# A dense mixture of experts on TensorE: 112 gathered tokens instead of 96, and the gathered sums on GpSimd

## The chip, the cores and the metric

The kernel runs on one core of one Trainium2 chip. The time is device microseconds (us) from the start to the end of one execution. The engines are PE (TensorE: matrix products), DVE (VectorE), ACT (ScalarE), POOL (GpSimd) and SP (SyncE, which here only issues DMAs). Each engine runs its own list of instructions in order; they wait for each other through semaphores.

## What is computed

The reference is two transformer-like blocks on 512 tokens of width 1024. The change sits almost wholly in the first block's expert layer. There are 16384 experts of one neuron each; every token picks 128 of them (8 heads, 16 each), and sums their outputs by a gate:

```python
    def block_fn(args):
        hb, ib, gb = args
        u = expert_down[ib]
        act = jax.nn.gelu(jnp.einsum("td,thkd->thk", hb, u), approximate=False)
        v = expert_up[ib]
        return jnp.einsum("thk,thkd->td", gb * act, v)
```

`hb` are the tokens, `ib` their expert numbers, `gb` the gates. The second block has, among other things, a linear attention, a state-space layer (S5) and a feed-forward layer.

## The kernel before

**Two ways to do the experts.** For most tokens (TD = 416) the kernel does all 16384 experts densely, as 128 blocks j of 128 experts, and multiplies by a gate that is zero for experts not picked. For the first TG = 96 tokens it gathers only the picked experts' rows from memory. `GROUPS` lists the gathered tokens as (first token, number of gathers, picks of a token in one gather): (0, 64, 2) and (64, 32, 4). Each gather fetches 128 rows of 1024 floats, 512 KB.

**Down stage** (loop over j, L815 to L826). `linear` loads the block `ed[j]`, splits it into a high and a low part (`hi` by ACT at L118, `lo` by DVE at L119; each in three buffers), and issues 24 matmuls of 128 x TD (L126, L127, L128). ACT applies the GELU and every second block goes to memory as `act_d`. After each block `run_fill` takes pieces of other work from a list: `select` (the top-k, on DVE), `scatter` (the dense gates of 8 tokens: three one-hot operations on DVE at L734, L737, L740, 16 matmuls at L745, ACT copies, and for every TC = 32 tokens a POOL DMA into `g_d`), `dot` (POOL gathers a `row` at L756, three buffers; DVE multiplies it with the tokens and sums, L764), `weigh` (GELU of the dots times gate) and the first NOW = 16 `add`s. An `add` gathers a row of `expert_up` on POOL (L756, the same three buffers) and DVE does `tsum += row * gate` in one instruction (L779).

**Up stage** (loop over j, L1050 to L1097). Per block ACT loads `aj` (two blocks of `act_d`) and for every eight blocks `gt` (their gates from `g_d`); `load_w` brings `eu[j]`; DVE forms `wg = aj * gt` (L1077), ACT and DVE split it into `wh` and `wl` (L131, L132), and 24 matmuls of 128 x 416 add into eight PSUM banks. The other 80 `add`s and the preparation of the second block (`s5_prepare`, `ada`) are in this stage's list. The last two blocks are held back, and after them small matmuls (L1097) add `tsum`.

**What sets the order.** A scheduler places the instructions of each engine; `soon()` gives the weight path priority, `issue_after` holds an instruction until a named one is issued, and `fill`'s costs and budgets say how much goes beside each block. What stands in the list of an engine is then run strictly in that order.

**Second block.** At L1397 SP loads the S5 inputs `u4` (8 DMAs for each of 8 parts) in the same queue as the weights; `tables` (L1403) and `carry` (L1435) are called in turn in the loop at L1493 to L1520.

## Time and profile before

| what | us |
|---|---|
| median of three runs (lowest, highest) | 2742.34 (2730.85, 2746.29) |
| the profiled execution | 2736.44 |
| its span in the trace | 2734.7 |
| PE busy | 2630.8 (96%) |
| DVE busy | 1874.4 (69%) |
| ACT busy | 1070.8 (39%) |
| POOL busy | 491.1 (18%) |
| down stage, 423 to 1102 us | 679 |
| up stage, 1107 to 1720 us | 613 |

The profiled execution's mean granted PE clock was 0.983 of full speed. Busy time of PE counts pipelined matmuls, so the distance between the starts of two matmuls, not the duration of one, is what a matmul costs. POOL's DMA issues count as busy where they are indirect (gathers). The rows are in a section of their own below.

### The profile page before, as it was taken

Reading aid. Unit: us, or ns where it says so; the run is one execution under the profiler, and the core shown is the slowest. Engines: PE = TensorE matmul, PEld = TensorE weight load, DVE = VectorE, ACT = ScalarE, POOL = GpSimd, SP = SyncE. Lnnn points to the kernel's source line nnn. Section 1 sums busy time; section 2 is a strip of 40 time slices with the busy share of each in tenths; the row PEclk is TensorE's granted clock in tenths of the full one; section 3 lists DMA queues with packets and bytes.
Section 4 is the critical chain, followed back from the end, with each engine's and each line's share of the span. In section 5 each row is a group of like instructions: output and inputs, shape, how many; then the busy total and the mean of one; then the engine's idle time right before and its main releaser. Section 6 shows DMA issues by size and latency. Waiting matters only on the chain.

```text
span 2734.7 us, 36390 instructions
## 1 busy us (share of the span) xinstructions
PE 2630.8 (96%) x13784; PEld 2349.5 (86%) x13784; DVE 1874.4 (69%) x3430; ACT 1070.8 (39%) x1510; POOL 491.1 (18%) x431
## 2 busy tenths in 40 slices
PE   6999999999999999999999899999999989999997
PEld 5777789999999999999899899877788878688886
DVE  5777699998998874788688576744456654562543
ACT  4564333434445444334433233544323243432221
POOL 0001000343343021224423120100002320010100
PEclk9999999999999999999999999999999999999999
DMA  6324424889888577979887887222265654233321
GB/s 255 101 87 139 144 93 133 282 286 327 301 307 323 188 263 259 313 273 339 297 319 265 281 302 258 82 63 70 70 193 177 191 159 132 72 98 96 97 96 66
DMA packets 182304, 532.95 MB, mean 195 GB/s; under 512 B 20592, under 2 KB 59472, under 8 KB 180208
## 3 DMA queue, kind: packets, MB, share of 16 engines
q1 hardware_dynamic: 89872, 282.57, 31.2%
q0 software_dynamic: 39952, 157.64, 16.5%
q10 hardware_dynamic: 52304, 90.41, 9.7%
q8 instruction: 108, 1.77, 0.3%
q14 instruction: 68, 0.56, 0.1%
HBM read 448.98 MB, written 80.41 MB: 194 GB/s over the span
## 4 chain that ended last, share of the span: by engine, by line
PE 84%; DMA 6%; DVE 5%; issue 2%; ACT 2%; POOL 1%; ACTq 0%; SPq 0%; DVEq 0%; POOLq 0%
PE ps L127 24%; PE ps L126 24%; PE ps L128 24%; PE ps L745 4%; DMA gt<-g_d 3%; DMA row<-in_eu_dram,gid 1%; DVE lo L119 1%; PE ps L1307 1%; PE ps L1310 1%; DVE wg L1077 1%; PE ps L615 1%; PE ps L148 0%; PE ps L1421 0%; ACT hi L118 0%; PE ps L487 0%
## 5 line engine op out<-in xcount | busy, mean ns | idle before, releaser
L118 ACT ACTIVATE hi<-raw 128x1024 fp32r<-128x1024 f32 (+2 forms) x459 | 481.3, 1051 | 1068.0 <-PE ps L127 796.9
L119 DVE TENSOR_TENSOR lo<-raw,hi 128x1024 fp32r<-128x1024 f32 (+2 forms) x459 | 579.4, 1264 | 347.6 <-ACT hi L118 319.1
L126 PE MATMUL ps<-h2h,hi 128*128 128x416 f32 (+1 forms) x1152 | 413.1, 360 | 3.9 <-ACT h2h L569 3.0
L127 PE MATMUL ps<-h2l,hi 128*128 128x416 f32 (+1 forms) x1152 | 413.1, 359 | 2.9 <-DVE h2l L570 2.9
L128 PE MATMUL ps<-h2h,lo 128*128 128x416 f32 (+1 forms) x1152 | 411.2, 358 | 0.0
L127 PE MATMUL ps<-wl,hi 128*128 128x416 f32 x1024 | 363.8, 355 | 11.4 <-DVE wl L132 11.4
L128 PE MATMUL ps<-wh,lo 128*128 128x416 f32 x1024 | 358.4, 357 | 10.9 <-DVE lo L119 10.9
L126 PE MATMUL ps<-wh,hi 128*128 128x416 f32 x1024 | 351.2, 355 | 6.6 <-ACT wh L131 4.5
L126 PE MATMUL ps<-Ah,hi 128*128 128x512 f32 (+2 forms) x944 | 337.7, 363 | 18.0 <-ACT Ah L131 7.0
L127 PE MATMUL ps<-Al,hi 128*128 128x512 f32 (+2 forms) x944 | 340.6, 361 | 2.7 <-DVE Al L1123 2.7
L128 PE MATMUL ps<-Ah,lo 128*128 128x512 f32 (+2 forms) x944 | 338.1, 359 | 0.5 <-DVE lo L119 0.5
L756 POOL DMA_INDIRECT row<-in_eu_dram,gid x96 | 181.9, 1895 | 398.5 <-DVE tsum L779 329.6
L126 PEld LDWEIGHTS ps<-h2h,hi 128*128 128x128 f32 x1152 | 218.0, 189 | 11.5 <-ACT h2h L569 3.8
L127 PEld LDWEIGHTS ps<-h2l,hi 128*128 128x128 f32 x1152 | 217.8, 189 | 9.9 <-DVE h2l L570 3.6
L128 PEld LDWEIGHTS ps<-h2h,lo 128*128 128x128 f32 x1152 | 217.8, 189 | 6.4
L126 PEld LDWEIGHTS ps<-Ah,hi 128*128 128x128 f32 x944 | 179.0, 191 | 50.0 <-ACT Ah L131 7.9
L127 PEld LDWEIGHTS ps<-wl,hi 128*128 128x128 f32 x1024 | 194.4, 190 | 16.6 <-DVE wl L132 13.0
L127 PEld LDWEIGHTS ps<-Al,hi 128*128 128x128 f32 x944 | 180.2, 191 | 32.6 <-issue 5.0
L128 PEld LDWEIGHTS ps<-wh,lo 128*128 128x128 f32 x1024 | 195.5, 191 | 13.1 <-DVE lo L119 11.9
L128 PEld LDWEIGHTS ps<-Ah,lo 128*128 128x128 f32 x944 | 179.6, 190 | 30.7 <-issue 6.0
L126 PEld LDWEIGHTS ps<-wh,hi 128*128 128x128 f32 x1024 | 196.0, 192 | 10.2 <-ACT wh L131 5.2
L756 POOL DMA_INDIRECT row<-in_ed_r_dram,gid x96 | 144.6, 1506 | 218.9 <-DVE dots L764 194.1
(602 smaller groups left out, 4199.5 us busy)
## 6 DMA issues: line engine op xcount, KB each, us to landing
raw<-in_ed_dram SPq DMA_DIRECT2D x128, 512.0 KB, 5.1
raw<-in_eu_dram SPq DMA_DIRECT2D x128, 512.0 KB, 5.5
raw<-in_win_dram SPq DMA_DIRECT2D x67, 512.0 KB, 3.6
raw<-in_wff_dram SPq DMA_DIRECT2D x64, 512.0 KB, 3.8
g_d<-gst POOLq DMA_DIRECT2D x13, 2048.0 KB, 9.7
aj<-act_d ACTq DMA_DIRECT2D x64, 416.0 KB, 4.5
wa<-in_wada_dram SPq DMA_DIRECT2D x46, 512.0 KB, 4.5
gt<-g_d ACTq DMA_DIRECT2D x45, 512.0 KB, 9.8
```

The lines of the kernel that those rows point to most:

```text
L118: top[0] = nc.scalar.activation(hi[:, :n], raw[:, :n], AF.Copy)
L119: low[0] = nc.vector.tensor_sub(lo[:, :n], raw[:, :n], hi[:, :n].bitcast(F32))
L126: nc.tensor.matmul(ps, wh, x[0], start=first, stop=False)
L127: nc.tensor.matmul(ps, wh, x[1], start=False, stop=False)
L128: nc.tensor.matmul(ps, wl, x[0], start=False, stop=last)
L615: nc.tensor.matmul(ps[:, t * P : t * P + P], q[:, t * P : t * P + P], skt[:, m], start=True, stop=True)
L745: nc.tensor.matmul(ps[:, i * P : i * P + P], o1[:, c, :, i], o2[a][:, c, :, i], start=a == 0, stop=a == 1)
L756: nc.gpsimd.indirect_dma_start(out=raw, out_offset=None, in_=src.rearrange("a b d -> (a b) d"), in_offset=bass.IndirectOffsetOnAxis(ap=gid ...
L1077: nc.vector.tensor_tensor(wg.rearrange("p (c t) -> p c t", t=TC), aj[:, j % 2].rearrange("p (c t) -> p c t", t=TC), gt[:, :, j % 8], ALU.mult)
L1307: nc.tensor.matmul(po[hs], qx[:, c * 64 : c * 64 + 64], st, start=False, stop=True)
L1310: nc.tensor.matmul(ps, kt[hs, j], vt[hs, j], start=True, stop=True)
```

## The change

**Groups and widths.** A third group (96, 16, 8) is gathered, so TG is 112 and TD 400. The gates are kept by TC = 24 tokens: 400 = 16 x 24 + 16, in 16 chunks of `g_d` and one smaller `ge_d`. `wg` becomes two DVE instructions (384 and 16 columns), `gt` gets a fifth, small DMA and is issued after the block j-8 instead of j-6.

**Sums.** An `add` is now a POOL gather, a POOL multiplication in place (`row * gate`) and a POOL addition (`tsum += row`), carried out one or two gathers after its own. No sum is left on DVE. NOW is 48: of these, 32 alternate with the dots of groups 1 and 2, and 16 come after all the dots. 64 stay for the up stage. `weigh(1)` and `weigh(2)` come after all the dots.

**The rest.** The first `aj` goes into two buffers of another pool (tag "tl", which the dots' `junk` uses too) through SP; `fill`'s budget goes over P-6 blocks with a cap of 4.8 instead of P-8 and 4.2; in S5 the `u4` loads go from SP's queue to POOL's, and `tables` is called after `carry`.

```diff
-    TC = 32
-    GROUPS = ((0, 64, 2), (64, 32, 4))
+    TC = 24
+    GROUPS = ((0, 64, 2), (64, 32, 4), (96, 16, 8))
...
-    NCH = TD // TC
+    NCH, TE = divmod(TD, TC)
...
+    ge_d = dp.tile([P, P, TE], F32, name="ge_d")
...
-            if i == 0:
-                tsum[g] = gx.tile([P, D], F32, tag=f"tok{g}", name=f"tsum{g}")
-                nc.vector.tensor_scalar(tsum[g], raw, w, None, ALU.mult)
-            else:
-                nc.vector.scalar_tensor_tensor(tsum[g], raw, w, tsum[g], ALU.mult, ALU.add)
...
+        def sums_of(lag):
+
+            while len(pending) > lag:
+                g, i, raw = pending.pop(0)
+                w = ggate[g][:, i : i + 1]
+                if g not in tsum:
+                    tsum[g] = gx.tile([P, D], F32, tag=f"tok{g}", name=f"tsum{g}")
+                    nc.gpsimd.tensor_scalar(tsum[g], raw, w, None, ALU.mult)
+                else:
+                    nc.gpsimd.tensor_scalar(raw, raw, w, None, ALU.mult)
+                    nc.gpsimd.tensor_tensor(tsum[g], tsum[g], raw, ALU.add)
+
+        def add(g, i, lag):
+            pending.append((g, i, fetch(I["eu"], g, i)))
+            sums_of(lag)
...
-        SPILL, NOW = 0, 16
+        NOW, LAST = 48, 16
+        adds = [(1.3, lambda p=p, n=n: add(*p, 1 if n < NOW else 2)) for n, p in enumerate(picks)]
...
+        down = [dot_of(p) for p in picks[:n0]] + [(0.1, lambda: weigh(0))]
+        dots_, adds_ = [dot_of(p) for p in picks[n0:]], adds[: NOW - LAST]
+        while dots_ or adds_:
+            for l in (dots_, adds_):
+                if l:
+                    down.append(l.pop(0))
+        down += [(0.1, lambda g=g: weigh(g)) for g in range(1, len(GROUPS))]
...
-        fill.extend(down)
-
-        per = sum(c for c, _ in fill) / (P - 8)
+        fill.extend(down + adds[NOW - LAST : NOW] + [(0.1, lambda: sums_of(0))])
+
+        per = sum(c for c, _ in fill) / (P - 6)
...
-            run_fill(min((j + 1) * per - done[0], 4.2))
+            run_fill(min((j + 1) * per - done[0], 4.8))
...
+            gathers = adds[NOW:] + [(0.1, lambda: sums_of(0))]
...
-                with tc.issue_after(tops[max(j - 6, 0)].ins) if j else ExitStack():
+                with tc.issue_after(tops[max(j - 8, 0)].ins) if j else ExitStack():
...
+                    nc.scalar.dma_start(ge[:, a:b], ge_d[:, j // 8 * 8 + a : j // 8 * 8 + b])
...
+                if j == 0:
+                    aj = [tp.tile([P, TD], F32, tag="tl", name=nm("aj"), bufs=3) for _ in range(2)]
+                    for i, a in enumerate(aj):
+                        nc.sync.dma_start(a, act_d[0][:, i * TD : i * TD + TD])
...
-                nc.vector.tensor_tensor(
-                    wg.rearrange("p (c t) -> p c t", t=TC), aj[:, j % 2].rearrange("p (c t) -> p c t", t=TC), gt[:, :, j % 8], ALU.mult)
+                v = lambda a: a[:, : NCH * TC].rearrange("p (c t) -> p c t", t=TC)
+                nc.vector.tensor_tensor(v(wg), v(aj[j % 2]), gt[:, :, j % 8], ALU.mult)
+                nc.vector.tensor_tensor(wg[:, NCH * TC :], aj[j % 2][:, NCH * TC :], ge[:, j % 8], ALU.mult)
...
-                        nc.sync.dma_start(u4[r0 : r0 + 16, 4 * m : 4 * m + 4], usrc[g, s])
+                        nc.gpsimd.dma_start(u4[r0 : r0 + 16, 4 * m : 4 * m + 4], usrc[g, s])
...
-            if gi % 2 == 0 and gi + 2 < NGR:
-                nxt = tables(gi // 2 + 1)
             if gi % 2 == 1:
                 sts = nxt
             cur, held = held, carry(gi + 1, sts) if gi + 1 < NGR else None
+            if gi % 2 == 0 and gi + 2 < NGR:
+                nxt = tables(gi // 2 + 1)
```

**DVE, from the down stage to the up stage.** In the kernel before, the list of DVE there reads as follows (`lo_10037` to `lo_10115` belong to the first three blocks of the up stage):

```order
L119 TENSOR_TENSOR lo_10037<-raw_10035,hi_10036 128x1024
L119 TENSOR_TENSOR lo_10073<-raw_10071,hi_10072 128x1024
L1077 TENSOR_TENSOR wg_10041<-aj_10033,gt_10028 128x416
L1077 TENSOR_TENSOR wg_10077<-aj_10033,gt_10028 128x416
L1031 TENSOR_REDUCE fold_10024<-ident 128x64
L1031 TENSOR_REDUCE fold_10026<-ident 128x32
L119 TENSOR_TENSOR lo_10115<-raw_10113,hi_10114 128x1024
L132 TENSOR_TENSOR wl_10043<-wg_10041,wh_10042 128x416
L132 TENSOR_TENSOR wl_10079<-wg_10077,wh_10078 128x416
L1077 TENSOR_TENSOR wg_10119<-aj_10111,gt_10028 128x416
```

The first `wg` stand behind weight splits alone. In the changed kernel (`lo_10166` is the last block of the down stage; `lo_10232`, `lo_10269` and `lo_10313` are the first three of the up stage; L767 is a dot, in two instructions) the list reads:

```order
L119 TENSOR_TENSOR lo_10166<-raw_10164,hi_10165 128x1024
L119 TENSOR_TENSOR lo_10232<-raw_10230,hi_10231 128x1024
L767 ISA junk_8833,dots_2368<-row_8831,htok_2365 128x1024
L767 ISA dots_2368 128x1
L119 TENSOR_TENSOR lo_10269<-raw_10267,hi_10268 128x1024
L1041 TENSOR_REDUCE fold_10214<-ident 128x64
L1041 TENSOR_REDUCE fold_10216<-ident 128x32
L1041 TENSOR_REDUCE fold_10218<-ident 128x16
L119 TENSOR_TENSOR lo_10313<-raw_10311,hi_10312 128x1024
L767 ISA junk_8903,dots_2368<-row_8901,htok_2365 128x1024
L767 ISA dots_2368 128x1
L767 ISA junk_9005,dots_2368<-row_9003,htok_2365 128x1024
```

and, 30 instructions further on, with the last of the third group's dots ahead:

```order
L767 ISA junk_9695,dots_2372<-row_9693,htok_2369 128x1024
L767 ISA dots_2372 128x1
L767 ISA junk_9761,dots_2372<-row_9759,htok_2369 128x1024
L767 ISA dots_2372 128x1
L771 TENSOR_TENSOR ggate_2371<-ggate_2371,dots_2372 128x16
L1091 TENSOR_TENSOR wg_10236<-aj_10226,gt_10220 128x384
L1092 TENSOR_TENSOR wg_10236<-aj_10226,gt_10220 128x16
L132 TENSOR_TENSOR wl_10238<-wg_10236,wh_10237 128x400
```

Between `lo_10313` and the first `wg` there now stand 18 dots (two of group 1, all 16 of group 2) and the instructions of `weigh`.

**POOL, at the same place.** In the changed kernel, the last gathers of the down stage (L759; `in_ed_r` for a dot, `in_eu` for a sum), with the multiplications (L786) and additions (L787) among them:

```order
L759 DMA row_9003<-in_ed_r_dram,gid_2366 128x1024
L759 DMA row_9069<-in_eu_dram,gid_2362 128x1024
L786 TENSOR_SCALAR row_8966<-row_8966,ggate_2363 128x1024
L759 DMA row_9073<-in_ed_r_dram,gid_2370 128x1024
L786 TENSOR_SCALAR row_9069<-row_9069,ggate_2363 128x1024
L787 TENSOR_TENSOR tsum_6630<-tsum_6630,row_8966 128x1024
L759 DMA row_9139<-in_ed_r_dram,gid_2370 128x1024
L759 DMA row_9176<-in_ed_r_dram,gid_2370 128x1024
L787 TENSOR_TENSOR tsum_6630<-tsum_6630,row_9069 128x1024
L759 DMA row_9241<-in_ed_r_dram,gid_2370 128x1024
L759 DMA row_9245<-in_ed_r_dram,gid_2370 128x1024
```

A sum's multiplication of `row_9069` stands behind its own gather and ahead of all but one of the third group's gathers (`gid_2370`).

**POOL, in the up stage.** Before, POOL only gathers there, and issues the DMAs of the S5 preparation (`mats_d`):

```order
L756 DMA row_11428<-in_eu_dram,gid_2361 128x1024
L756 DMA row_11467<-in_eu_dram,gid_2361 128x1024
L985 DMA mats_d<-bd_10195 128x8x128
L985 DMA mats_d<-bd_10196 128x8x128
L756 DMA row_11595<-in_eu_dram,gid_2361 128x1024
L985 DMA mats_d<-bd_10195 128x8x128
L985 DMA mats_d<-bd_10196 128x8x128
L756 DMA row_11598<-in_eu_dram,gid_2361 128x1024
L756 DMA row_11637<-in_eu_dram,gid_2361 128x1024
```

Now, gathers, multiplications and additions follow each other:

```order
L759 DMA row_9939<-in_eu_dram,gid_2362 128x1024
L759 DMA row_9943<-in_eu_dram,gid_2362 128x1024
L786 TENSOR_SCALAR row_9902<-row_9902,ggate_2363 128x1024
L787 TENSOR_TENSOR tsum_6630<-tsum_6630,row_9902 128x1024
L786 TENSOR_SCALAR row_9939<-row_9939,ggate_2363 128x1024
L759 DMA row_9947<-in_eu_dram,gid_2362 128x1024
L786 TENSOR_SCALAR row_9943<-row_9943,ggate_2363 128x1024
L787 TENSOR_TENSOR tsum_6630<-tsum_6630,row_9939 128x1024
L786 TENSOR_SCALAR row_9947<-row_9947,ggate_2363 128x1024
L787 TENSOR_TENSOR tsum_6630<-tsum_6630,row_9943 128x1024
L759 DMA row_9984<-in_eu_dram,gid_2362 128x1024
L787 TENSOR_TENSOR tsum_6630<-tsum_6630,row_9947 128x1024
```

The addition of a row stands up to two rows behind its gather; the multiplication is often right behind one.

## Rows read from the trace of the kernel before

**Rows 1.** Windows: stretch, length, busy us (x instructions) by engine, PE clock, DMA share, GB/s.

```profile
423.00:1102.00 679.00, 678.13 (x3922) 658.43 (x3921) 566.17 (x952) 307.43 (x385) 188.82 (x142) 1.00 0.77 270
1102.00:1107.00 5.00, 0.86 (x5) 0.52 (x3) 1.05 (x3) 1.48 (x2) 0.00 (x0) 0.82 0.84 284
1107.00:1720.00 613.00, 588.19 (x3049) 577.62 (x3050) 468.06 (x776) 212.69 (x292) 174.80 (x97) 0.98 0.85 291
```

**Rows 2.** Chain that ended last: start us, length us, what; four of its pieces.

```profile
956.81 1.91 PE ps L745 x16
...
1102.90 3.03 DMA aj<-act_d
...
1519.59 27.26 DMA row<-in_eu_dram,gid
...
1610.71 17.51 DMA gt<-g_d
```

**Rows 3.** Timeline of PE in the up stage: start us, us, instruction; eight issues apart.

```profile
1129.65 0.35 PE L128 MATMUL ps<-wh,lo 128*128 128x416 f32 x1
...
1131.15 0.35 PE L127 MATMUL ps<-wl,hi 128*128 128x416 f32 x1
```

**Rows 4.** The same view at 512 columns, eight issues apart.

```profile
2299.73 0.39 PE L128 MATMUL ps<-Ah,lo 128*128 128x512 f32 x1
...
2301.54 0.39 PE L127 MATMUL ps<-Al,hi 128*128 128x512 f32 x1
```

**Rows 5.** Groups by line, whole span: count | busy us, mean ns | idle before, releaser.

```profile
L756 POOL DMA_INDIRECT row<-in_eu_dram,gid x96 | 181.9, 1895 | 398.5 <-DVE tsum L779 329.6 <-DMA row<-in_eu_dram,gid 14.2 <-DVE s5e L876 14.0
...
L756 POOL DMA_INDIRECT row<-in_ed_r_dram,gid x96 | 144.6, 1506 | 218.9 <-DVE dots L764 194.1 <-DVE pi L666 8.9 <-issue 4.6
...
L764 DVE CUSTOM_DVE_ANT_0 junk<-row,htok 128x1024 bf16<-128x1024 f32 x96 | 116.0, 1218 | 21.4 <-DMA row<-in_ed_r_dram,gid 21.3
...
L950 POOL MEMSET bd<- 128x1024 f32 x2 | 1.9, 984 | 0.0
```

**Rows 6.** The same grouping for DVE in the up stage alone, 1107 to 1720 us.

```profile
L779 DVE SCALAR_TENSOR_TENSOR tsum<-row,ggate,tsum 128x1024 f32<-128x1024 f32 x79 | 100.9, 1278 | 15.9 <-DMA row<-in_eu_dram,gid 15.9
...
L1077 DVE TENSOR_TENSOR wg<-aj,gt 128x416 f32<-128x416 f32 x127 | 69.7, 584 | 50.3 <-DMA gt<-g_d 36.9 <-issue 9.2 <-DMA aj<-act_d 4.1
...
L219 DVE DVE_READ_ACCUMULATOR2_ANT mod<- 128x1 f32 x8 | 0.7, 82 | 0.0
```

**Rows 7.** Timelines of PE, ACT and DVE where the down stage ends and up begins.

```profile
1102.52 0.34 PE L128 MATMUL ps<-h2h,lo 128*128 128x416 f32 x1
...
1107.18 2.10 PE L126 MATMUL ps<-wh,hi 128*128 128x416 f32 x5 [4.32 <-ACT wh L131]
...
1103.35 1.06 ACT L118 ACTIVATE hi<-raw 128x1024 fp32r<-128x1024 f32 x1 [3.65 <-PE ps L128]
...
1105.95 1.09 DVE L1077 TENSOR_TENSOR wg<-aj,gt 128x416 f32<-128x416 f32 x2 [5.40 <-DMA aj<-act_d]
```

**Rows 8.** Timelines of POOL and DVE in the feed-forward stage: start us, us, instruction.

```profile
2437.77 1.04 POOL L1591 TENSOR_TENSOR f<-f 128x512 f32<-128x512 f32 x1 [4.40 <-ACT hi L118]
...
2437.80 2.09 DVE L119 TENSOR_TENSOR lo<-raw,hi 128x1024 fp32r<-128x1024 f32 x1 [0.18 <-ACT hi L118]
...
2465.18 1.23 DVE L119 TENSOR_TENSOR lo<-raw,hi 128x1024 fp32r<-128x1024 f32 x1 [4.24 <-ACT hi L118]
```

**Rows 9.** DMA issues: queue, count, KB each, median us from issue to landing.

```profile
raw<-in_ed_dram SPq DMA_DIRECT2D x128, 512.0 KB, 5.1
...
gt<-g_d ACTq DMA_DIRECT2D x45, 512.0 KB, 9.8
...
row<-in_ed_r_dram,gid POOLq DMA_INDIRECT x96, 6.9
...
row<-in_eu_dram,gid POOLq DMA_INDIRECT x96, 8.0
```

**Rows 10.** Chain again, at the start of the second block's S5 stage.

```profile
2026.26 1.08 SPq L1397
...
2028.84 3.94 DMA raw<-in_win_dram
```

More of the change, by code (lines that the diff above doesn't have):

```diff
@@ L727, in scatter @@
             if off == 0:
-                gst[ch] = px.tile([P, P, TC], F32, tag="g", name=nm("gst"))
+                gst[ch] = px.tile([P, P * TC], F32, tag="g", name=nm("gst"))
+            tc_ = TC if ch < NCH else TE
+            to = gst[ch][:, : P * tc_].rearrange("p (j t) -> p j t", t=tc_)
             n = SC // 4
@@ L746, in scatter @@
                 nc.scalar.copy(
-                    gst[ch][:, :, off + 4 * c : off + 4 * c + 4].rearrange("p j t -> p t j"), ps.rearrange("p (t j) -> p t j", j=P))
-            if off + SC == TC:
-                nc.gpsimd.dma_start(g_d[ch], gst[ch])
+                    to[:, :, off + 4 * c : off + 4 * c + 4].rearrange("p j t -> p t j"), ps.rearrange("p (t j) -> p t j", j=P))
+            if off + SC == tc_:
+                nc.gpsimd.dma_start(g_d[ch] if ch < NCH else ge_d, to)
         picks = [(g, i) for g, (_, n, _) in enumerate(GROUPS) for i in range(n)]
@@ L770, in tile_blocks @@
         tsum = {}
-        def add(g, i):
-            raw = fetch(I["eu"], g, i)
-            w = ggate[g][:, i : i + 1]
-            if i == 0:
-                tsum[g] = gx.tile([P, D], F32, tag=f"tok{g}", name=f"tsum{g}")
-                nc.vector.tensor_scalar(tsum[g], raw, w, None, ALU.mult)
-            else:
-                nc.vector.scalar_tensor_tensor(tsum[g], raw, w, tsum[g], ALU.mult, ALU.add)
-        def later(fn):
-            with tc.issue_after(low[0].ins):
-                fn()
+        pending = []
+        def sums_of(lag):
[11 more added lines that the diff above has]
+            sums_of(lag)
         dot_of = lambda p: (1.4, lambda p=p: dot(*p))
-        adds = [(1.3, lambda p=p: later(lambda: add(*p))) for p in picks]
-        SPILL, NOW = 0, 16
+        NOW, LAST = 48, 16
+        adds = [(1.3, lambda p=p, n=n: add(*p, 1 if n < NOW else 2)) for n, p in enumerate(picks)]
         select(0)
@@ L797, in tile_blocks @@
         todo, fill[:] = fill[:], []
-        dotted = []
-        for g, (_, n, _) in enumerate(GROUPS):
-            dotted += [dot_of(p) for p in picks if p[0] == g]
-            dotted.append((0.1, lambda g=g: weigh(g)))
-        cut = len(dotted) - SPILL - 1 if SPILL else len(dotted)
-        down, left = dotted[:cut], dotted[cut:]
-        down += adds[:NOW]
+        n0 = GROUPS[0][1]
+        down = [dot_of(p) for p in picks[:n0]] + [(0.1, lambda: weigh(0))]
[5 more added lines that the diff above has]
+        down += [(0.1, lambda g=g: weigh(g)) for g in range(1, len(GROUPS))]
         share = sum(c for c, _ in down) / sum(c for c, _ in todo)
@@ L1040, in beside @@
             fill.clear()
-            of_first = GROUPS[0][1]
-            gathers = []
-            for i, a in enumerate(adds[NOW:of_first]):
-                gathers.append(a)
-                if left and i % 2 == 1:
-                    gathers.append(left.pop(0))
-            gathers += left + adds[max(of_first, NOW) :]
+            gathers = adds[NOW:] + [(0.1, lambda: sums_of(0))]
             share = sum(c for c, _ in gathers) / sum(c for c, _ in rest)
@@ L1067, in tile_blocks @@
                         nc.scalar.dma_start(gt[:, c:c1, a:b], g_d[c:c1, :, j // 8 * 8 + a : j // 8 * 8 + b].rearrange("c p j t -> p c j t"))
+                    nc.scalar.dma_start(ge[:, a:b], ge_d[:, j // 8 * 8 + a : j // 8 * 8 + b])
             if j % 2 == 0:
-                aj = px.tile([P, 2, TD], F32, tag="act", name=nm("aj"))
-                nc.scalar.dma_start(aj.rearrange("p a t -> p (a t)"), act_d[j // 2])
+                if j == 0:
+                    aj = [tp.tile([P, TD], F32, tag="tl", name=nm("aj"), bufs=3) for _ in range(2)]
+                    for i, a in enumerate(aj):
+                        nc.sync.dma_start(a, act_d[0][:, i * TD : i * TD + TD])
+                else:
+                    at_ = px.tile([P, 2, TD], F32, tag="act", name=nm("aj"))
+                    nc.scalar.dma_start(at_.rearrange("p a t -> p (a t)"), act_d[j // 2])
+                    aj = [at_[:, i] for i in range(2)]
             w = load_w(I["eu"][j])
```

4 lines of the change are left out of this document (3 added, 1 removed).

## The prediction

> **What bounds the kernel now.** I read the windows first. In the down stage (423 to 1102 us) PE is busy for 678 of 679 us, DVE for 566 and POOL for 189; in the up stage PE for 588 of 613, DVE for 468 and POOL for 175 [rows 1]. So PE sets both stages, and DVE is the next engine. How much a matmul costs is the distance of two starts: eight take 1131.15 - 1129.65 = 1.50 us at 416 columns, 0.1875 each [rows 3]. A stage has 128 x 24 = 3072 of them, 576 us. In the down stage 832 scatter matmuls at 1.91 / 16 = 0.119 [rows 2] add 99, in all 675 of 679. In the up stage 613 - 576 = 37 us are not matmul pace. The chain shows where most of it goes: gate tiles that landed late (17.5 us for `gt<-g_d` at 1610) and once a gathered row for which DVE waited (27 us at 1519) [rows 2]. Between the stages PE stands still from 1102.52 to 1107.18, 4.67 us, because the first `wg` waits for `aj` [rows 2, 7].
>
> **The narrower dense part (a gain).** At 512 columns eight matmuls take 1.81 us, 0.2263 each [rows 4]. The slope is (0.2263 - 0.1875) / 96 = 0.0004 us a column; 16 columns are 0.0065 us, by plain proportion 0.0072, so 20 to 22 us in each stage: 21. Two scatters fewer are 32 x 0.119 = 4 us, down only. That is -25 in the down stage and -21 in the up stage before anything is late, on PE, which sets both ends.
>
> **The price of a sum on POOL.** DVE did it in 1.28 us [rows 6]. Now POOL does two instructions on 128x1024. An addition of 128x512 took POOL 1.04 us [rows 8], so 2.08 at twice the size. A multiplication by one value a row has no row on POOL: it lies between a fill of the same size, 0.98 [rows 5], and the addition's 2.08. I take 1.1, nearest to the fill, since it has one input where the addition has two. A sum is 3.2 us (3.06 to 4.16).
>
> **POOL holds DVE up.** In the feed-forward stage a weight split on DVE that starts 0.03 us behind a POOL addition takes 2.09 us, and 1.23 where POOL is idle; it ends 1.08 us after the addition's end, as if it had begun only then [rows 8]. Nearly all of DVE's work in both stages (weight splits, dots, `wg`, `wl`) also has two inputs in SBUF. So I count POOL's additions, and its multiplications too, as time taken from DVE. The Trainium skill ("SBUF — State Buffer", section "Who interferes with whom") says that a DVE instruction with two SBUF inputs contends with a GpSimd instruction that reads SBUF, and that whichever is first holds the shared port pair for its whole instruction; the trace agrees for the addition (2.09 against 1.23), and no row of it shows a multiplication. By that page moving the sums off DVE would take nothing off the shared port; it would more than double their share of it.
>
> **Down stage.** DVE keeps about its 566 us: 16 dots more at 1.22 [rows 5] are +20, 16 sums fewer at 1.28 are -20. Some 30 of the 48 early sums run on POOL before the end, 30 x 3.2 = 96. 566 + 96 = 662 against PE's 679 - 25 = 654: 8 us late (0 where they interleave well without multiplications blocking, 25 where the sums come in lumps). **Down: -25 + 8 = -17.**
>
> **The seam between the stages (a loss).** This is the largest term and is read from the order of the changed kernel. `lo_10313`, the third block of the up stage, uses the weight buffer of the last down block, so its `hi` can begin only when PE has finished; before, that `hi` also began at 1103.35, right behind PE's last down matmul [rows 7]. All 16 dots of the third group and two more now stand behind it on DVE, and behind those the first `wg`. PE's next matmul needs that `wg`, so all 18 dots are on the path. Their gathers are not ahead either: three row buffers are freed only by these dots. Step by step from PE's stop: `hi` and `lo` are done after 3 us, the first dot (1.22) after 4.3. Only then can POOL issue the gather of the sum `row_9069`, whose buffer that dot frees. POOL's next instructions but one gather wait for it: it lands 8.0 us later [rows 9], at 12.3, multiplication and addition take 3.2, to 15.5. Then the dot of `row_9139` is done 6.9 (landing [rows 9]) + 1.2 later, 23.6. The 14 dots left go through three buffers, each buffer once in 6.9 + 1.2 = 8.1 us: 14 x 8.1 / 3 = 38, to 61. `wg`, `wh` and the weighing add 2: 63 us. These landings are medians under load. While PE stands still the weight loads stop, so landings should be nearer to the 5.1 us of a plain load of the same 512 KB [rows 9]: the same steps then give 4.3 + 5.1 + 3.2 + 6.3 + 14 x 6.3 / 3 + 2 = 50. I take 55. The new `aj` load through SP waits for the junk buffers of the third and second last dot, so it lands about with the last dot and adds little. Before, the seam cost 4.67. **Seam: +50** (45 to 58). What was fetched ahead of the stop (three weight blocks) saves nothing, since the up stage is not short of weights.
>
> **Up stage.** PE needs 576 - 21 = 555. DVE loses the sums, 468 - 101 = 367 [rows 1, 6]; `wg` and `wl` are 16 columns shorter, 256 x 0.584 x 16 / 416 = -6; 128 small second `wg` at about the 0.08 of DVE's smallest instruction [rows 6] are +10: 371. POOL has 16 + 64 sums, 80 x 3.2 = 256. Taken in turns that is 627 us, more than PE's 555: the stage goes by DVE and POOL. With the multiplication at 2.08 it would be 371 + 333 = 704; if nothing of POOL's work held DVE up, PE's 555 and what is left of the 37 us. Issuing `gt` two blocks (some 9 us) earlier takes a part of each 12 to 17 us landing, and DVE no longer waits for rows: 580 for that end. I take 627. **Up: 627 - 613 = +14** (-33 to +91).
>
> **Second block.** The S5 loads leave SP's queue. Before, a weight load stood behind them and its 3.94 us was on the chain [rows 10]; on POOL they stand behind each part's own store. Between the gain of that wait (-5) and as much lost by POOL being late (+5): **-2**.
>
> **Sum.** -17 + 50 + 14 - 2 = +45 against the profiled execution's 2736.4: **2781 us**. The median of the runs shown is 6 us above that execution; I leave this out of the forecast and compare with the median, 2742.3, where 0.5% (14 us, about what a measurement of this kernel can tell from no change) is 2728.6 to 2756.
>
> **Rivals.** *B, the sums hide.* If the multiplication (one tensor input) does not hold DVE up, DVE and the additions need 371 + 80 x 2.08 = 537 in the up stage, under PE's 555, and 566 + 62 = 628 under 654 in the down stage. Then up is 580 and down is free: -25 + 50 - 33 - 2 = -10, 2726; with half of the gt stalls left some 2740. For it: no row shows a multiplication that blocks. Against: it reads SBUF as the addition does. Range 2712 to 2752.
>
> *C, the seam is short as well: faster.* The seam's floor is POOL's issue of gathers, 16 x 1.5 [rows 5] = 24, with the 9 us ahead of it 33, instead of 55. It decides where landing and dot together take under 3 x 1.5 = 4.5 us, a landing of about 3.3; the shortest median in [rows 9] is 5.1. With B's stages: -25 + 28 - 33 - 2 = -32, **2704**. If the seam alone were short, with the ports binding: 2759.
>
> *D, POOL cannot keep up.* In the up stage many multiplications stand right behind their own gather. Its issues and sums are 80 x (1.9 + 3.2) = 408 us [rows 5]; where 35 of the multiplications wait out a whole landing of 8.0 [rows 9], POOL needs 688, 75 more than the 613, and its sums end the stage, since the last small matmuls need `tsum`. A multiplication at 2.08 gives about the same, 704. Time 2736 - 17 + 50 + 75 - 2 = **2842**, from 2825 up. Against it: three row buffers let a gather run under the sums of the two before.
>
> **How the numbers follow.** Forecast 0.50 (2755 to 2825): the seam is read from the order and needs no unknown price, and the port's hold is seen in a row. B 0.24, C 0.13, D 0.10, something else 0.03. The range 2705 to 2830 leaves out D, half of C and a little more. Faster: C and a third of B, 0.21. Same: the rest of B, 0.17. Slower: the forecast and D, 0.62. The forecast's own range is 2755 to 2825.
>
> **What would show it.** In the profile after: PE idle for 50 to 60 us at the end of the down stage, released by `wh` behind the dots, with DVE waiting there for `row<-in_ed_r`; a PE pace of 0.181 us a matmul in both stages; weight splits on DVE of over 2 us wherever a POOL sum runs; an up stage of about 627 us whose PE waits are for `lo`, `wl` or `wg` and less for `gt`. If the seam is under 35 us, or splits beside a POOL multiplication take 1.2, the forecast is wrong by that term.

## The result and the profile after

The changed kernel takes 2929.4 us (median), the kernel before 2741.4: the ratio is 1.0685, with a 95% interval of 1.0639 to 1.0731. Forecast were 2781 (2705 to 2830). The sign was right, the size was not: +188 us instead of +45. One of the changed kernel's four executions took 5127 us; it counts in this median and not in the ratio, and the other three took 2924 to 2934 us. The profiled execution has a span of 2922.2 us, 187.5 more than before.

Where the 187.5 us lie is read from the starts of PE's matmuls, which divide the program in the same way in both traces (us):

| stretch | before | after | difference | forecast |
|---|---|---|---|---|
| up to the end of the scores, ahead of the down stage | 429.2 | 424.7 | -4.5 | 0 |
| down stage, to its last matmul | 673.3 | 667.8 | -5.5 | -17 |
| seam, to the first matmul of the up stage | 4.7 | 70.6 | +66.0 | +50 |
| up stage, to the first small matmul with tsum | 611.3 | 707.7 | +96.4 | +14 (with the next line) |
| those small matmuls | 10.0 | 57.1 | +47.1 | |
| the rest, second block | 1006.2 | 994.2 | -12.0 | -2 |

The 4.5 us of the first line look like chance for the most part: the kernel below with the second block's part alone has there the program of the kernel before, and takes 426.1 us for it.

The windows of the changed kernel (columns as in [rows 1]: length, then busy us of PE, weight loads, DVE, ACT, POOL; granted clock; DMA share; GB/s) are the down stage, the seam, the up stage, the small matmuls, and two stretches out of the up stage:

```profile
425.00:1092.00 667.00, 649.42 (x3852) 631.33 (x3852) 597.95 (x887) 325.55 (x374) 364.71 (x225) 0.99 0.79 276
1092.00:1163.00 71.00, 0.81 (x5) 0.49 (x3) 34.03 (x47) 3.82 (x7) 48.06 (x34) 0.52 0.72 240
1163.00:1871.00 708.00, 600.32 (x3040) 584.07 (x3041) 610.34 (x818) 207.43 (x290) 519.74 (x235) 0.92 0.73 241
1871.00:1928.00 57.00, 12.88 (x83) 12.77 (x81) 4.95 (x6) 3.81 (x6) 46.41 (x23) 0.61 0.28 90
1200.00:1300.00 100.00, 70.96 (x336) 68.44 (x337) 92.56 (x158) 20.74 (x31) 71.46 (x34) 0.84 0.63 201
1300.00:1400.00 100.00, 92.97 (x484) 90.93 (x483) 83.47 (x106) 39.49 (x57) 53.88 (x28) 0.95 0.79 258
```

In the up stage DVE is busy for 610 us of 708, where [rows 1] had 468 of 613, although 80 sums of 1.28 us have left it. Of the last two stretches PE comes to 336 matmuls in the one where DVE is busy for 93 of 100 us, and to 484 in the one where DVE is busy for 83. From the seam to the end of the up stage PE waits for DVE, and at the end for POOL (total us, times, longest):

```profile
PE ps L127 <- DVE wl L132: 93.8, 34, 13.0
PE ps L126 <- ACT wh L131: 70.7, 2, 70.3
PE ps L1111 <- POOL tsum L787: 44.1, 1, 44.1
PE ps L128 <- DVE lo L119: 13.2, 8, 2.5
```

The second line is the seam, the third is a small matmul that waits for the last sums. The gate tiles of [rows 2] have not gone: in the chain two of them still stand with 13.28 us (at 1435) and 13.15 (at 1478). From 1634 us to the end of the small matmuls the chain goes through POOL's gathers, multiplications and additions. The groups by line show what a sum costs on POOL (count, busy us, mean ns, idle before); they answer to the rows on L756 and L779 in [rows 5, 6]:

```profile
L786 POOL TENSOR_SCALAR row<-row,ggate 128x1024 f32<-128x1024 f32 x109 | 342.7, 3146 | 56.6 <-DMA row<-in_eu_dram,gid 54.6
L787 POOL TENSOR_TENSOR tsum<-tsum,row 128x1024 f32<-128x1024 f32 x109 | 279.7, 2566 | 3.0
```

Where DVE stood idle, while PE waited for the last sum, POOL's timeline gives the undisturbed prices, and the wait for the gather's landing:

```profile
1894.85 2.84 POOL L786 TENSOR_SCALAR row<-row,ggate 128x1024 f32<-128x1024 f32 x1 [0.97 <-DMA row<-in_eu_dram,gid]
1897.86 1.01 POOL L759 DMA_INDIRECT row<-in_eu_dram,gid  x1 [0.17 <-issue]
1898.90 2.35 POOL L787 TENSOR_TENSOR tsum<-tsum,row 128x1024 f32<-128x1024 f32 x1
```

So a sum is 2.84 + 2.35 = 5.19 us of POOL alone, and 5.7 in the mean, beside DVE's work.

### The profile page after: what moved, and what is told of

It is laid out like the page before. It is cut to its first block, busy times and chain, and to the rows that moved or that the text cites. A ratio compares the mean times of both kernels' runs of the same rounds, so it can differ in the third digit from the quotient of the medians.

```text
span 2922.2 us, 36616 instructions
## 1 busy us (share of the span) xinstructions
PE 2619.7 (90%) x13768; PEld 2337.5 (80%) x13768; DVE 2089.8 (72%) x3488; ACT 1089.9 (37%) x1507; POOL 1141.5 (39%) x776
## 4 chain that ended last, share of the span: by engine, by line
PE 61%; DVE 14%; DMA 10%; POOL 7%; issue 5%; ACT 2%; ACTq 1%; SPq 0%; DVEq 0%; POOLq 0%
PE ps L127 17%; PE ps L126 17%; PE ps L128 17%; DMA row<-in_eu_dram,gid 4%; POOL row L786 3%; PE ps L748 3%; DVE lo L119 3%; DMA row<-in_ed_r_dram,gid 3%; POOL tsum L787 2%; DVE wl L132 1%; DVE wg L1092 1%; DVE wg L1091 1%; DMA gt<-g_d 1%; POOL row L759 1%; DVE junk L767 1%
## 5 line engine op out<-in xcount | busy, mean ns | idle before, releaser
L119 DVE TENSOR_TENSOR lo<-raw,hi 128x1024 fp32r<-128x1024 f32 (+2 forms) x459 | 632.5, 1380 | 344.5 <-ACT hi L118 323.1
L127 PE MATMUL ps<-wl,hi 128*128 128x400 f32 x1024 | 371.8, 363 | 93.9 <-DVE wl L132 93.8
L126 PE MATMUL ps<-wh,hi 128*128 128x400 f32 x1024 | 364.5, 359 | 70.8 <-ACT wh L131 70.7
L126 PE MATMUL ps<-h2h,hi 128*128 128x400 f32 (+1 forms) x1152 | 405.3, 353 | 6.9 <-ACT hi L118 3.9
L128 PE MATMUL ps<-h2h,lo 128*128 128x400 f32 (+1 forms) x1152 | 403.6, 351 | 6.8 <-DVE lo L119 6.8
L127 PE MATMUL ps<-h2l,hi 128*128 128x400 f32 (+1 forms) x1152 | 405.4, 352 | 2.9 <-DVE h2l L571 2.9
L128 PE MATMUL ps<-wh,lo 128*128 128x400 f32 x1024 | 364.9, 358 | 13.2 <-DVE lo L119 13.2
L786 POOL TENSOR_SCALAR row<-row,ggate 128x1024 f32<-128x1024 f32 x109 | 342.7, 3146 | 56.6 <-DMA row<-in_eu_dram,gid 54.6
L787 POOL TENSOR_TENSOR tsum<-tsum,row 128x1024 f32<-128x1024 f32 x109 | 279.7, 2566 | 3.0
L759 POOL DMA_INDIRECT row<-in_ed_r_dram,gid x112 | 157.8, 1409 | 202.6 <-DVE dots L767 156.5
```

The costliest lines, as they stand in the source:

```text
L119: low[0] = nc.vector.tensor_sub(lo[:, :n], raw[:, :n], hi[:, :n].bitcast(F32))
L126: nc.tensor.matmul(ps, wh, x[0], start=first, stop=False)
L127: nc.tensor.matmul(ps, wh, x[1], start=False, stop=False)
L128: nc.tensor.matmul(ps, wl, x[0], start=False, stop=last)
L759: nc.gpsimd.indirect_dma_start(out=raw, out_offset=None, in_=src.rearrange("a b d -> (a b) d"), in_offset=bass.IndirectOffsetOnAxis(ap=gid ...
L786: nc.gpsimd.tensor_scalar(raw, raw, w, None, ALU.mult)
```

## Experiments

The first theory was: POOL's chain of gather, multiplication and addition is too long for the up stage, and its additions hold DVE up; the seam is the dots that stand on DVE behind the last weight split. Where no ratio is given, a time is of a single execution, beside which the kernel before took 2737 to 2740 us (single or median).

**The multiplication left out.**

```diff
-                    nc.gpsimd.tensor_scalar(raw, raw, w, None, ALU.mult)
                     nc.gpsimd.tensor_tensor(tsum[g], tsum[g], raw, ALU.add)
```

> The changed kernel without the multiplication of a gathered row by its gate on POOL: the rows are added as they are (part of the sum is left out). In the changed kernel PE stood still 70.6 us at the seam, the up stage from its first matmul to the first fold matmul took 707.7 us, and PE waited 44 us more for tsum. Theory (POOL's own chain is too long, because the multiplication takes 2.84 us, and its additions hold DVE): the wait for tsum falls under 5 us, the up stage to 610 to 650 us; by the order 13 dots are left at the seam instead of 18, so 40 to 55 us there; whole time 2760 to 2800 us. Rival 1 (only the hold of the port on DVE matters, POOL's length does not): the additions are still there, so the up stage stays at 680 to 710. Rival 2 (POOL waits for its own gathers to land): the up stage and the wait for tsum stay within 15 us of what they were.

Measured: 2878.4 us. The wait for tsum is gone (the small matmuls take 11.3 us instead of 57.1), so the multiplication's length is what makes POOL end last. But the up stage is 733.7 us, 26 longer than with the multiplication and above even rival 1's bracket: the additions alone make it long. With the small matmuls it is 745.0 us against the 764.8 of the changed kernel, so the multiplication costs 20 us on top of them. Where it need not wait, POOL now does a gather and an addition every 3.6 us, and DVE gets what is left:

```profile
1501.53 0.96 POOL L759 DMA_INDIRECT row<-in_eu_dram,gid  x1 [0.27 <-POOL tsum L786]
1502.51 2.35 POOL L786 TENSOR_TENSOR tsum<-tsum,row 128x1024 f32<-128x1024 f32 x1
1505.13 0.96 POOL L759 DMA_INDIRECT row<-in_eu_dram,gid  x1 [0.27 <-POOL tsum L786]
1506.11 2.35 POOL L786 TENSOR_TENSOR tsum<-tsum,row 128x1024 f32<-128x1024 f32 x1
```

**The additions left out.**

```diff
                     nc.gpsimd.tensor_scalar(raw, raw, w, None, ALU.mult)
-                    nc.gpsimd.tensor_tensor(tsum[g], tsum[g], raw, ALU.add)
```

> The changed kernel without the additions on POOL: each row is gathered and multiplied in place, and tsum holds only the first product (part of the sum is left out). Theory (a multiplication takes 2.84 us of POOL but holds DVE little; the addition is what holds DVE): DVE's busy time in the up stage falls from 610 to 380 to 430 us, no wait for tsum, the up stage 580 to 610 us, whole time 2750 to 2790 with a seam of 50 to 60 (16 dots by the order). Rival (the multiplication holds DVE as the addition does): DVE busy stays over 500 us and the up stage over 640.

Measured: 2738.6 us, up stage 604.7, no wait for tsum, DVE busy for 445 us of the up stage (a little over the bracket, under the rival's), seam 48.6. It is faster than forecast because the down stage came down as well, to 651.3 from 667.8. So the 80 additions of the up stage cost 707.7 - 604.7 = 103 us there, 1.3 us each. With the multiplications alone the stage is 3.5 us longer than with the sums on DVE (601.2, the next kernel). They do hold DVE: there its own work is 468.6 us less 78 sums of 1.28, some 369, so that 76 of the 445 us are theirs, nearly 1 us each; but DVE has that room. Four hundred us of this up stage, and the same of the changed kernel's (1989 matmuls against 1637):

```profile
1200.00:1600.00 400.00, 370.97 (x1989) 361.44 (x1989) 300.29 (x502) 141.39 (x198) 286.86 (x136) 0.98 0.89 303
...
1200.00:1600.00 400.00, 327.57 (x1637) 316.21 (x1638) 358.64 (x511) 120.06 (x172) 289.15 (x136) 0.91 0.72 237
```

In both POOL is busy for some 72%; without the additions PE hardly feels it.

**All sums back on DVE, the lists as in the change.**

```diff
-                    nc.gpsimd.tensor_scalar(raw, raw, w, None, ALU.mult)
-                    nc.gpsimd.tensor_tensor(tsum[g], tsum[g], raw, ALU.add)
+                    nc.vector.scalar_tensor_tensor(tsum[g], raw, w, tsum[g], ALU.mult, ALU.add)
```

> The changed kernel with every sum given back to DVE (one instruction, row times gate plus tsum, as before), all else and all lists as in the change: 112 gathered tokens, 48 early sums. By the order 8 dots stand at the seam instead of 18. Theory (POOL's sums make the up stage long): no wait for tsum, the up stage 580 to 615 us, the seam 25 to 40 us, whole time 2720 to 2760 us. Rival (the 16 tokens more, with their gathers and the narrower gate tiles, cost the time, whoever sums): up stage over 660 us, whole time over 2820.

Measured: 2713.9 us, 23 less than the kernel before beside it. Down stage 650.0, seam 29.0, up stage 601.2: as expected, but for 6 us at the whole. The rest of the change is no loss; the sums on POOL are. The 18 us more in the changed kernel's down stage (667.8) are theirs as well.

**The dots first.**

```diff
-        while dots_ or adds_:
-            for l in (dots_, adds_):
-                if l:
-                    down.append(l.pop(0))
-        down += [(0.1, lambda g=g: weigh(g)) for g in range(1, len(GROUPS))]
+        down += dots_ + [(0.1, lambda g=g: weigh(g)) for g in range(1, len(GROUPS))] + adds_
```

> The changed kernel with the order of the down stage's list changed alone: all dots, both weighings, then the sums, where the changed kernel alternates 32 sums with the dots. By the order no dot stands between the last weight split and the first wg. Theory (the seam is the dots that stand behind the last weight split on DVE): PE stands still under 12 us at the seam instead of 70.6; the sums move into the up stage unchanged, so up stage and wait for tsum together stay at 750 to 800 us; whole time 2850 to 2890 us. Rival (POOL is the bound from the middle of the down stage on, and the seam is only where its lateness shows): what the seam gives back comes again as a wait for tsum, and the whole time stays within 15 us of 2924.

Measured: 2983.1 us. The seam falls to 6.9 us, as the theory wants; but only 13 sums are done before the up stage, where the changed kernel had 32, and the 99 left take until the small matmuls have waited 180 us:

```profile
PE ps L1107 <- POOL tsum L787: 179.6, 2, 102.4
PE ps L127 <- DVE wl L132: 74.6, 30, 6.3
```

Neither bracket held it, though the rival was right that the seam's gain comes again as a wait for tsum. From the first matmul of the up stage to the last small one there are 900.4 us for 99 sums, 9.1 each; in the changed kernel 764.8 for 80, 9.6 each. So in both POOL makes one sum in 9 to 10 us. In the changed kernel 5.7 of the 9.6 are its two instructions, 1.3 the gather's issue, and the rest mostly waits for landings (46.9 us in all) and for S5's matrix stores, which stand in its queue (90.1 us in nine waits and 28.2 in one):

```profile
POOL mats_d L995 <- ACT bd L993: 90.1, 9, 52.9
POOL row L786 <- DMA row<-in_eu_dram,gid: 46.9, 20, 14.7
POOL mats_d L1018 <- DVE s5e L886: 28.2, 1, 28.2
```

**The seam over five kernels.** It is 70.6 us with 18 dots behind the last weight split (the change), 48.6 with 16, 40.3 with 13, 29.0 with 8, 6.9 with none: 2.6 to 2.8 us a dot above those 6.9, and 3.5 in the changed kernel, where sums stand among the gathers. The kernels below with 13 or 14 dots there take 41 to 45 us, the one with 18 takes 68.5, and those with none 5.5 to 10.9; the last one, with 4 dots and a `scatter`, takes 34.6.

**The kernel before with the sums on POOL alone** (96 gathered tokens, gates by 32). The edit is the part of the change's diff with `sums_of` and the new `add`, with `adds` written as

```diff
-        adds = [(1.3, lambda p=p: later(lambda: add(*p))) for p in picks]
+        adds = [(1.3, lambda p=p, n=n: add(*p, 1 if n < 16 else 2)) for n, p in enumerate(picks)]
```

> The kernel before (96 gathered tokens, gates by 32, 16 early sums) with only the sums moved to POOL as in the change, one or two gathers behind. By the order no dot stands at the seam. Theory (POOL's additions hold DVE, and its chain of gather, multiplication and addition ends the stage): up stage and wait for tsum together 100 to 170 us longer than before, whole time 2830 to 2910 us. Rival (the long up stage of the changed kernel came from the narrower gates or the 16 tokens more): under 2780.

Measured: 2858.6 us, 119 more than the kernel before beside it. The up stage is 724.3, 113 longer than before; no wait for tsum, seam 10.9. The move of the sums does by itself most of what the change lost (119 of 188 us). POOL's chain does not end the stage here, as the theory had it: 69 sums were left at its start, and the last was done 37 us ahead of the first small matmul. What is long is the up stage itself.

**The additions in quarters.**

```diff
-                    nc.gpsimd.tensor_scalar(raw, raw, w, None, ALU.mult)
-                    nc.gpsimd.tensor_tensor(tsum[g], tsum[g], raw, ALU.add)
+                    for q in range(4):
+                        s_ = slice(q * 256, q * 256 + 256)
+                        nc.gpsimd.tensor_tensor(tsum[g][:, s_], tsum[g][:, s_], raw[:, s_], ALU.add)
```

> The kernel e3_no_mult (no multiplication on POOL; that part of the sum is left out) with each addition in four of 256 columns: the same work on POOL in shorter pieces. e3_no_mult had an up stage of 733.7 us and 2878 us in all. Theory (an instruction of DVE that comes behind an addition waits for its whole 2.35 us, however small it is itself, so the length of one hold counts): the up stage falls to 600 to 670 us, whole time 2750 to 2820. Rival (the port's total time counts, not the length of one hold): up stage 715 to 755 us, whole time 2860 to 2900.

Measured: 2870.5 us, up stage 727.5. The theory, that the length of one hold counts, has fallen, and the rival's brackets held. That the sum of the holds counts is not shown by this: four pieces take POOL 3.57 us where the whole took 2.46, and with 106 us more of additions (375 against 268, down stage included) the up stage was no longer.

**The additions spread out.** Two kernels, both without the multiplication: with the stores on ACT's queue and each addition tied to a block, and with the stores alone.

```diff
+                    if tick[0] is not None:
+                        nc.gpsimd.tensor_copy(gx.tile([P, 1], F32, tag="seen", name=nm("seen"), bufs=2), tick[0])
                     nc.gpsimd.tensor_tensor(tsum[g], tsum[g], raw, ALU.add)
...
-            nc.gpsimd.dma_start(mats_d[:, ps_, o_ : o_ + P], to)
+            nc.scalar.dma_start(mats_d[:, ps_, o_ : o_ + P], to)
...
+                tick[0] = gx.tile([P, 1], F32, tag="tick", name=nm("tick"), bufs=16)
+                nc.scalar.copy(tick[0], wh[:, :1].bitcast(F32))
```

> The kernel e3_no_mult (no multiplication on POOL; that part of the sum is left out; up stage 733.7 us), with two edits: before each addition of the up stage POOL reads one number that ACT writes once in each block j, so the additions cannot run ahead of the blocks beside which they were placed; and the S5 preparation's matrix stores go through ACT's queue, so POOL does not wait for them and then catch up. Theory (the additions come in lumps, and only in a lump does DVE fall behind PE, since POOL's 80 x 2.35 = 188 us spread evenly leave DVE 371 + 188 = 559 of the 555 us that PE needs): up stage 590 to 650 us. Rival (each addition that DVE meets costs PE time wherever it stands): up stage 690 us or more.

> The same kernel with the second edit alone: the S5 preparation's matrix stores through ACT's queue, no pacing (the multiplication is left out as in e3_no_mult). Theory (POOL runs its sums as fast as rows land, so they lump whether or not a store holds them up): up stage 690 to 740 us. Rival (the lumps came from the stores): up stage under 660.

Measured: 2845.8 us and 2882.0; up stages 705.5 and 745.2 (without either edit 733.7). The additions were indeed spread, 7 to 9 in each 50 us for 400 us and a few after. It brought 28 to 40 us, not the 80 and more of the theory, and the rival's bracket held: lumps are the smaller part. (All are single executions; the kernel with the constant, below, has an up stage 24 us longer than the changed kernel's.) Four hundred us of the paced kernel show where the rest is:

```profile
1180.00:1580.00 400.00, 311.14 (x1513) 297.00 (x1513) 361.68 (x463) 124.33 (x221) 263.52 (x160) 0.91 0.77 251
```

DVE is busy for 362 of 400 us. Sums and the S5 preparation lie in the same two thirds of the stage, so that DVE's own work and the holds together nearly fill it there, and PE gets 1513 matmuls instead of the 1989 of the kernel without additions. The 559 us for the whole stage left out where DVE's work lies. How far a still better spread would come was not tried.

**Multiplication by a constant**, to see whether the per-row gate makes it slow.

```diff
-                    nc.gpsimd.tensor_scalar(raw, raw, w, None, ALU.mult)
+                    nc.gpsimd.tensor_scalar(raw, raw, 0.5, None, ALU.mult)
```

> The changed kernel with POOL's multiplication by a constant 0.5 in place of the row's gate (the sums are then not weighted by the gates, except the first product of a group). By the order 18 dots stand at the seam, as in the changed kernel. In the changed kernel an undisturbed multiplication took 2.84 us, more than the addition's 2.35. Theory (reading one value per row from memory is what makes it slow): 1.0 to 1.6 us with a constant, no wait for tsum over 10 us, whole time 2860 to 2900 us. Rival (any multiplication of 128x1024 by one value takes POOL that long): 2.7 to 2.9 us, whole time 2910 to 2945 us.

Measured: 2914.9 us; the shortest multiplication 2.77 us, mean 2.93 (3.15 with the gate). The rival holds: on this shape POOL multiplies by one value more slowly than it adds two tensors, wherever the value comes from:

```profile
L786 POOL TENSOR_SCALAR row<-row 128x1024 f32<-128x1024 f32 x109 | 318.5, 2925 | 50.3 <-DMA row<-in_eu_dram,gid 48.9
```

The up stage is 732.1 us and the wait for tsum 10.6, against 707.7 and 44.1 with the gate; with the small matmuls the stage is 755.8 and 764.8. So the up stage by itself can differ by 24 us between kernels that differ in little, and not much rests on the 26 us by which it was longer without the multiplication.

**The second block's part alone**, on the kernel before.

```diff
-                        nc.sync.dma_start(u4[r0 : r0 + 16, 4 * m : 4 * m + 4], usrc[g, s])
+                        nc.gpsimd.dma_start(u4[r0 : r0 + 16, 4 * m : 4 * m + 4], usrc[g, s])
...
-            if gi % 2 == 0 and gi + 2 < NGR:
-                nxt = tables(gi // 2 + 1)
             if gi % 2 == 1:
                 sts = nxt
             cur, held = held, carry(gi + 1, sts) if gi + 1 < NGR else None
+            if gi % 2 == 0 and gi + 2 < NGR:
+                nxt = tables(gi // 2 + 1)
```

> The kernel before with only the second block's part of the change: the u4 loads on POOL's queue and tables after carry. In the profile of the changed kernel the stretch from the last fold matmul to the feed-forward's norm is 11.7 us shorter than before (971.2 against 982.9). Theory (that is this edit): 8 to 14 us faster than before, and the PE stops of 4.57, 3.81 and 4.04 us in that stretch are gone. Rival (the gain came with what POOL and SP had left over from the longer up stage): within 5 us of before.

Measured: 2726.5 us, ratio 0.9946 (0.9929 to 0.9962); the stretch is 969.8 us instead of 982.9, and the three stops of PE, of which [rows 10] shows the first one's cause, are gone.

**What is worth keeping of the change:** the sums on DVE in the lists of the kernel before, with the narrower dense part and the second block's edit.

> The changed kernel with the sums on DVE and the lists, budgets and the 16 early sums of the kernel before: what is left of the change is 112 gathered tokens, gates by 24, gt two blocks earlier, the first aj through SP, and the second block's edit. By the order no dot stands at the seam. Theory: down stage 648 to 656 us, seam about 5, up stage 595 to 612, second block as in the changed kernel; whole time 2680 to 2705 us. Rival (the seam and up stage suffer from the 16 gathers more, whatever the order): over 2720.

Measured: 2689.9 us, ratio to the kernel before 0.9824 (0.9800 to 0.9848), 1.8% faster than the kernel before. Its down stage, seam and up stage:

```profile
427.00:1077.00 650.00, 647.16 (x3863) 629.32 (x3862) 573.04 (x956) 330.38 (x379) 222.54 (x178) 1.00 0.82 293
1077.00:1082.50 5.50, 0.36 (x3) 0.08 (x1) 1.49 (x4) 2.23 (x4) 0.00 (x0) 0.87 1.09 349
1082.50:1684.00 601.50, 568.61 (x3038) 563.04 (x3039) 487.56 (x912) 210.83 (x289) 170.95 (x113) 0.97 0.88 305
```

**16 tokens more still:**

```diff
-    GROUPS = ((0, 64, 2), (64, 32, 4), (96, 16, 8))
+    GROUPS = ((0, 64, 2), (64, 32, 4), (96, 16, 8), (112, 16, 8))
```

> The kernel e7_width_s5 with 16 more gathered tokens: 128, so 384 dense columns and no second gate tile. Theory (PE sets both stages as long as the sums are on DVE): 20 us less in each stage, minus what is left at the seam (by the order 4 dots and one scatter, 15 to 25 us): 2660 to 2690 us, against 2689.9. Rival (DVE, with 16 dots and 16 sums more, becomes the bound of a stage): over 2700.

Measured: 2703.1 us, ratio to the kernel before 0.9865 (0.9833 to 0.9897): not better than 112, whose interval it overlaps, and over the theory's bracket. The down stage falls by 34 us to 615.7, but the seam is 34.6 instead of 5.5, and the up stage 617.6 instead of 601.6, with DVE busy for 507 us of it, so not full. Five sums, not 16, were done before the up stage. That the dots and sums of 16 tokens more no longer fit beside PE's work is likely, but no run shows it.

## Why the prediction was wrong, step by step

**The narrower dense part** was right: 0.1816 us a matmul was measured (forecast 0.181), and with the sums on DVE the down stage is 649 to 650 us, 23 to 24 less than before (forecast 25). In the up stage, with the sums on DVE, 10 of the 21 us showed (601.2 and 601.6 against 611.3); more stops of PE took the rest.

**The price of a sum on POOL is a step that failed.** Taken was 3.2 us, bounded by 3.06 and 4.16; measured were 5.19 alone and 5.7 in the mean. The addition was near (2.35 against 2.08 from doubling the 128x512 row of [rows 8]). The multiplication was taken at 1.1 between a fill and the addition; it is 2.84, outside the bound. The bound rested on the belief that one tensor input cannot be slower than two; no row of before showed it, and it is not so here. Of POOL's 9.6 us a sum in the changed kernel, 2.5 are that mis-sizing, and 1.5 are the waits for S5's stores (118 us), which the working put at nothing. POOL then ends the stage, with a wait for tsum, as in rival D (from 2825 up, chance 0.10). D's own reason did not come true: it had 35 waits for landings of 8.0 us, 280 us, and they were 46.9.

**POOL holds DVE up: right for the addition, wrong for the multiplication.** In the changed kernel's timelines a weight split that starts 0.15 us into an addition takes 3.36 us and ends 1.09 after the addition, as in [rows 8]; one that starts 1.16 us into a multiplication takes its plain 1.21, and one that starts 0.43 us into one takes 1.76, though the multiplication runs on for 0.66 us after it has ended (timelines of POOL and DVE, a row of each for the three cases):

```profile
1700.25 2.42 POOL L787 TENSOR_TENSOR tsum<-tsum,row 128x1024 f32<-128x1024 f32 x1
...
1700.40 3.36 DVE L119 TENSOR_TENSOR lo<-raw,hi 128x1024 fp32r<-128x1024 f32 x1 [0.52 <-ACT hi L118]
...
1763.44 2.85 POOL L786 TENSOR_SCALAR row<-row,ggate 128x1024 f32<-128x1024 f32 x1
...
1764.60 1.21 DVE L119 TENSOR_TENSOR lo<-raw,hi 128x1024 fp32r<-128x1024 f32 x1
...
1800.68 2.85 POOL L786 TENSOR_SCALAR row<-row,ggate 128x1024 f32<-128x1024 f32 x1 [3.17 <-DMA row<-in_eu_dram,gid]
...
1801.11 1.76 DVE L119 TENSOR_TENSOR lo<-raw,hi 128x1024 fp32r<-128x1024 f32 x1 [2.17 <-ACT hi L118]
```

So the multiplication holds such a split up for about its first microsecond. The other splits of the trace agree: those that start 0.1 to 0.74 us into a multiplication of plain length all end 0.66 us before it, those that start 1.1 us in or later take 1.21 to 1.23. The Trainium skill ("SBUF — State Buffer", section "Who interferes with whom") says that a DVE instruction with two SBUF inputs contends with a GpSimd instruction that reads SBUF, and that the shared port pair is an exclusive lock. That the lock is held for the whole GpSimd instruction is so here for the addition and not for the multiplication.

**Up stage: the step from demand to time failed, and it weighs more.** "Taken in turns" made the stage as long as DVE's work and POOL's together, 371 + 256 = 627 us. The demand came out near, DVE being busy for 610 us, but partly by luck: the addition held DVE for longer than priced, and the multiplication, priced at 1.1 us, held it for about 1 us of its 2.84. The stage and its small matmuls took 764.8 us. Without the multiplication, where POOL does not end the stage, the demand is 371 + 80 x 2.35 = 559 us and DVE was busy for 575; yet the stage took 733.7, so a cheap multiplication would not have saved the forecast. The step supposes that DVE's work and POOL's additions are spread alike over the stage. They are not, as four hundred us of that kernel and what comes after them show:

```profile
1178.00:1578.00 400.00, 311.44 (x1484) 302.74 (x1485) 358.98 (x472) 111.62 (x157) 249.40 (x142) 0.86 0.75 248
1578.00:1864.00 286.00, 262.01 (x1408) 259.70 (x1407) 173.83 (x283) 88.23 (x118) 34.45 (x18) 0.96 0.69 226
```

In the stretch where both lie, DVE is busy for nine tenths, and PE comes to 3.7 matmuls a us; behind it PE comes to 4.9, and the time lost is not made up. A nearly full DVE is not the whole of it: from 1700 to 1800 us of the changed kernel DVE is busy for only 78 us, and PE comes to 390 matmuls. There the chain goes through POOL; what else held PE up was not tested. PE's stops come with a lower clock: the granted clock of the up stage is 0.92 against 0.98 [rows 1], and the 261 matmuls that stand 0.25 to 0.45 us apart instead of 0.18 (most of them 0.33), as at the lower of its two levels (1.2 GHz), cost 38 us of the 707.7, against 64 and 9 us before. Rival B's idea, that only the additions hold DVE up, was nearly right; its conclusion, that the sums would then hide, was wrong for the same reason as the forecast.

**The seam** was seen in the right place and for the right reason, and cost +66 us instead of +50 (45 to 58). By the steps of the working: `hi` and `lo` were to be done 3 us after PE's stop and were at 9.3, POOL having held the split (3.33 us); the first dot was to be done at 4.3 and was at 16.4: DVE waited for its row to land, and an addition that ran beside it made it 3.73 us long. The dot of `row_9139` was to be done at 23.6 and was at 35.4, behind the sums in POOL's queue. The last 14 took 33.6 us, between the 29 and 38 of the two landings, and what follows them 1.7. The failed price of a sum carried over into this term; the rhythm of the three buffers was right.

**Down stage:** 8 us were allowed for holds (0 to 25), 18 were measured (667.8 against 650.0 with the same lists and the sums on DVE).

**Second block:** -12 instead of -2. The three stops of PE were in the profile with 12.4 us together; the working weighed only the first and set a loss on POOL against it that did not come.

Of the difference between +188 and +45 the up stage with its small matmuls has 130 us, the seam 16. The rest, the down stage, the second block and what lies ahead of both, nearly cancels. Rival D came nearest in time, 2842, but from the same too cheap multiplication and from waits that did not come; its mechanism accounts for the wait for tsum, not for the long up stage.

## What to carry to other kernels

Work moved from DVE to POOL need not be off DVE: here an addition on POOL held DVE's two-input instructions up to its end (2.35 us), a multiplication for about 1 us. Count such holds into DVE's load stretch by stretch, not over a whole stage, and look for the place where both are dense. A price for an instruction form that no trace shows has no upper bound from a neighbouring form; one run of that form alone is worth more than any interpolation. When many small pieces are to be hidden, look in the order of instructions for the pieces that are left behind the last instruction that can still be covered: here 2.6 to 3.5 us for every dot.

## What the runs showed of the hardware that was not expected

POOL's multiplication of 128x1024 by one value took 2.84 us alone, with a constant 2.77, more than the addition of two such tensors (2.35). An addition in four pieces of 256 columns took 0.89 us a piece in the mean, 3.6 us in all against 2.46 for the whole, and the up stage was as long. Small DVE instructions can be held as long as large ones: one of 128x32 with a single tensor input, 0.17 us where nothing holds it, started 1.4 us into a multiplication and ended with the addition after it, 3.76 us later. Weight splits that start so late into a multiplication are not held by it, as shown above; nine of 15 such small instructions were. Why these differ was not tested.

```profile
1194.67 3.76 DVE L867 TENSOR_SCALAR s_xr<-s_x 128x32 f32<-128x32 f32 x1
```
